# Expert weights in 4-MB units: rows of 32768 bytes over fours of slots

## The chip, the core and the metric

The kernel runs on one core of one Trainium2 chip. Its engines work in parallel and each takes its own instructions strictly in order: TensorE (PE in the profile, PEld for its weight loads), VectorE (DVE), ScalarE (ACT), GpSimd (POOL) and SyncE (SP), which here only issues DMAs. The metric is the device time of one execution in microseconds (us). Three runs of the kernel before took 1317.88 to 1318.74 us, median 1318.44 us.

## The reference, cut to what matters

A decoder layer: a mixer (a state-space branch and a gated branch), cross-attention into 256 memory tokens, and a mixture of 32 experts, each followed by a layer norm. The change concerns the experts, which hold nearly all the weights:

```python
def moe(x, w_router, b_router, w_gu, b_gu, w_down, b_down):
    ...
    top_v, top_i = lax.top_k(logits, TOP_K)          # 4 of 32 for each of 256 tokens
    top_w = jax.nn.softmax(top_v, axis=-1)
    gates = jnp.sum(jax.nn.one_hot(top_i, N_EXPERTS, dtype=f32) * top_w[..., None], axis=1)
    def expert_step(acc, p):
        wgu, bgu, wd, bd, g = p                      # 1024x2048 and 1024x1024, float32
        hgu = xt @ wgu + bgu
        gate = jnp.minimum(hgu[:, :D_EXPERT], SWIGLU_LIMIT)
        up = jnp.clip(hgu[:, D_EXPERT:], -SWIGLU_LIMIT, SWIGLU_LIMIT)
        glu = gate * jax.nn.sigmoid(SWIGLU_ALPHA * gate)
        y = ((up + 1.0) * glu) @ wd + bd
        return acc + g[:, None] * y.astype(f32), None
```

One expert has 8 MB of gate-and-up weights and 4 MB of down weights: 384 MB in all, read once.

## The kernel before

**Two stages.** The first stage (to about 390 us) computes the mixer, the attention and the router. The second runs over the experts e = 0 to 31 in pairs. For each pair, one-hot matrices pick up to 64 tokens for each expert (`gather`, L971, in four groups of two 128-row blocks). An expert then has eight steps k of `products` (L1050: four products in each, against 2 x 512 gate and 2 x 512 up columns), the bias (L1057, four short products), `swiglu` on VectorE and ScalarE (L1062 to L1066), the transpose of its result `uc` (`hidden_t`, L1075, copied to `hT` by ScalarE in L1076), and `down` (L1089, eight steps of two products). After every odd expert `scatter` (L1100) adds both results of the pair to the sum. At expert 16, `add_rest` (L930, L937) adds the biases and the residual to it. The profile counts two instructions for each product in float32.

**Overlap.** The code starts the next expert early: after `swiglu` of expert e it issues the products of k = 0 and 1 of expert e + 1 (`AHEAD = 2`), and only then `hidden_t` and `down` of e. The final order of instructions on each engine is not that of the code: a scheduler chooses it at build time, from its own estimate of when each operand is there, the weights' DMAs among them. It may put a transpose ahead of products that it expects to wait for their weights.

**Weights.** Memory holds 22 slots of 1 MB (128 partitions x 8192 bytes). 14 are in one tile, `arena`; the pairs `xhl`, `ab`, `t01` and `t23` are tiles of a pool; `d` is half of `cd`. In the first stage these slots hold activations and that stage's own weights. Each call of `expert_w` fetches a unit of 2 MB on SP's queue. The first 22 MB come as 1-MB pieces (L1023, list `FIRST`), each into a slot that the first stage has given up. After that a unit goes to the next of ten pairs of slots (`RING`, L1035), as one DMA with rows of 16384 bytes; it waits until the products that read the pair's old contents are done. `products` calls `expert_w` in every second step, `down` twice. The last expert's down weights are cut by output columns (`w_last`), and the last units come as 1-MB pieces (L1033).

SP's queue is in order, and a DMA also waits for the one eight places ahead of it, so that at most eight are under way:

```python
        name = RING[(i - len(FIRST) // 2) % len(RING)]
        ...
        if apart:
            for h in range(2):
                nc.sync.dma_start(t[:, h], src[:, h])
        else:
            nc.sync.dma_start(t, src)
```

Of the kernel before, what the change touches and what calls it, by code (L numbers as in the profile page):

```python
# [17 lines left out]
P = 128  # L18
# [31 lines left out]
def block_kernel(ctx: ExitStack, tc: tile.TileContext, a, out):  # L50
# [11 lines left out]

    arena = cp.tile([P, len(SLOTS), 2048], F32, name="arena")
    big = ctx.enter_context(tc.tile_pool(name="big", bufs=1))

    def two(tag, dt=F32):

        return big.tile([P, 2, 2048], dt, tag=tag, name=uniq(tag))

# [133 lines left out]
    def w_parts():  # L203
        t = two(("t01", "t23")[tcount[0] % 2], F32R).rearrange("p q (i c) -> p q i c", i=2)
        tcount[0] += 1
        return [[t[:, q, i] for q in range(2)] for i in range(2)]
# [122 lines left out]
    kT = bt("e0").rearrange("p (k m) -> p k m", k=KB)  # L329
    mh, ml = feat("ab")  # L330
    hs, ls = w_parts()
# [30 lines left out]
    keys(2, wk2)  # L362
    xh, xl = feat("xhl")
    for k2 in range(4):
# [18 lines left out]

    gbm = bt("g").rearrange("p (g d) -> p g d", g=2)
    gvu = two("ab")
    gv = gvu[:, 0].rearrange("p (c d) -> p c d", c=2)
    st = stats_tile(2)
# [18 lines left out]
    ygh, ygl = feat("cd")  # L406
    uT = gvu[:, 1].rearrange("p (k t) -> p k t", k=KB)

# [190 lines left out]

    ysh, ysl = feat("ab")  # L600

# [93 lines left out]
    proj_residual(hh, hl, x0, x1, st)  # L695
    xh, xl = feat("xhl")
    bg3 = bgs[:96, :].bitcast(BF16)
# [308 lines left out]
    def expert_w(src, apart=False):

        i = ucount[0]
        ucount[0] += 1
        if 2 * i < len(FIRST):  # L1010
            t = []
            for h in range(2):
                name = FIRST[2 * i + h]
                with tc.issue_after(wload[PHASE_A.index(FIRST_AFTER.get(name, ("wo", 3)))].ins):
                    if name in SLOTS:
                        t.append(bt(name))
                    elif name == "d":
                        t.append(cd[:, 1])
                    else:
                        if h == 0:  # L1020
                            both = two(name)
                        t.append(both[:, h])
                    nc.sync.dma_start(t[h], src[:, h])  # L1023
            return t
        name = RING[(i - len(FIRST) // 2) % len(RING)]
        if name in SLOTS:
            at = SLOTS.index(name)
            t = arena[:, at:at + 2, :]
        else:
            t = two(name)  # L1030
        if apart:
            for h in range(2):
                nc.sync.dma_start(t[:, h], src[:, h])  # L1033
        else:
            nc.sync.dma_start(t, src)  # L1035
        return [t[:, h] for h in range(2)]

    def gate_up(src, sel, xe, before=None, last=False):

# [38 lines left out]

    def down(src, odd, hT, y, apart=False, between=None):

        for u in range(2):
            if u and between is not None:
                between()
            w = expert_w(src(u), apart)
            for b in range(4):
                k = 4 * u + b
                for n in range(2):
                    o = 64 * (n ^ odd)
                    te.matmul(y[n][o:o + 64, :], hT[:, b, 64 * u:64 * u + 64],  # L1089
                              w[b // 2][:, b % 2 * D + n * 512:b % 2 * D + (n + 1) * 512], start=(k == 0), stop=(k == KB - 1))  # L1090

# [74 lines left out]
    def before(e, k):  # L1166
# [12 lines left out]
        if e % 2 and k == 5 and e < NE - 1:  # L1179
            p.weights()  # L1180

    def begin(e):
        xg = pairs[e // 2].xg
        current[e] = gate_up(lambda u: a["w_gu"][e, u], i96[:, e:e + 1], lambda k: xg[:, k, e % 2 * CAP:(e % 2 + 1) * CAP],
                             lambda k: before(e, k), e == NE - 1)

# [3 lines left out]
    for e in range(NE - 2):  # L1190
        products, swiglu = current.pop(e)
        for k in range(AHEAD, KB):
            products(k)
        uc = swiglu()
        begin(e + 1)
        for k in range(AHEAD):
            current[e + 1][0](k)
        hT = hidden_t(uc)
        if e == 14:
            overflow_table()  # L1200
        if e == 16:
# [6 lines left out]
        down(lambda u: a["w_down"][e, u], b, hT, y)  # L1208
# [17 lines left out]
    hTb = []  # L1226
    down(lambda u: a["w_down"][ea, u], 0, hT, y, True, lambda: hTb.append(hidden_t(uc)))
    scatter_one(y, PS[0])
    ys = None
    for q in range(4):  # L1230
        if q % 2 == 0:
            w = expert_w(a["w_last"][q // 2], True)
        new = down_piece(hTb[0], w[q % 2], q)
        if ys is not None:
            scatter_piece(ys, PS[1], q - 1, st)
        ys = new
# [5 lines left out]
    with tc.For_i(0, nx, 1):  # L1242
# [49 lines left out]
        for i in range(2):  # L1292
# [14 lines left out]
RING = FIRST[0:20:2]  # L1307

# [15 lines left out]
def arrange(inputs):  # L1324
# [33 lines left out]
    r["w_last"] = wd[NE - 1].reshape(KB, P, 4, 256).transpose(2, 1, 0, 3).reshape(2, 2, P, 2 * D).transpose(0, 2, 1, 3)  # L1358
    r["b_gu"], r["b_down"] = I["b_gu"][0], I["b_down"][0]
# [21 lines left out]
```

## Time and profile before

| | |
|---|---|
| median of three runs | 1318.44 us (1317.88 to 1318.74) |
| profiled execution | 1318.8 us |
| its span, from first to last instruction | 1317.1 us |
| TensorE busy | 1254.6 us, 95% |
| mean granted clock | 0.987 of 2.4 GHz |
| DMA, whole span | 472.00 MB, 358 GB/s |
| second stage, first product to last | 393.6 to 1305 us |

The profile shows when each instruction ran on its engine, what a waiting instruction waited for, the clock that TensorE was granted, and how busy the DMA engines were. The span lies 1.7 us under the execution's own time. A busy TensorE is one with an instruction in flight; whether it or the weights set the pace of a stretch is read from what it waits for there.

### The profile page before, as it was taken

To read this page: it belongs to the slowest core of one execution; us is meant where nothing else is said; L and a number is where in the kernel's file an instruction comes from. 1 tells how busy PE (TensorE), PEld (TensorE's weight loads), DVE (VectorE), ACT (ScalarE), POOL (GpSimd) and SP (SyncE) were. 2 spreads that over 40 slices of the span, in tenths; PEclk is the share of its full clock that TensorE was granted. 3 is DMA by queue.
4 is the path that set the end of the run, shared out by engine and by line. 5 is a ranking of instruction groups with operands and counts; after the bars stand their busy time and mean duration, and the time that the engine had idled before them with its cause. 6 is when DMAs were issued, how large, how long until landed. Compare 5 with 4: busy or idle time off the path is not lost.

```text
span 1317.1 us, 15917 instructions
## 1 busy us (share of the span) xinstructions
PE 1254.6 (95%) x6767; PEld 686.7 (52%) x6768; DVE 451.4 (34%) x795; ACT 315.6 (24%) x536; POOL 28.6 (2%) x49
## 2 busy tenths in 40 slices
PE   6999999999999999999999999999999999989896
PEld 6899899989874343343333433333343433323232
DVE  4569766687441222121221122221221212202114
ACT  4746665544531111111111111101111111101000
POOL 2110000001000000000000000000000000000000
PEclk9999999999999999999999999969999999999998
DMA  9755543576789999999999999999999999999993
GB/s 356 242 175 195 192 160 133 193 289 225 277 315 362 422 425 428 427 427 428 427 427 428 429 428 427 412 427 427 426 429 428 427 428 426 427 427 428 429 421 134
DMA packets 43930, 472.00 MB, mean 358 GB/s; under 512 B 5104, under 2 KB 6928, under 8 KB 10064
## 3 DMA queue, kind: packets, MB, share of 16 engines
q1 hardware_dynamic: 39840, 464.41, 85.8%
q10 hardware_dynamic: 4016, 6.55, 1.6%
q8 instruction: 54, 0.88, 0.3%
q14 instruction: 20, 0.16, 0.0%
HBM read 469.49 MB, written 1.05 MB: 357 GB/s over the span
## 4 chain that ended last, share of the span: by engine, by line
PE 78%; DMA 15%; DVE 3%; ACT 2%; issue 1%; POOL 0%; ACTq 0%; DVEq 0%; SPq 0%; POOLq 0%
PE gu L1050 27%; PE y L1089 14%; PE mm L255 6%; PE mm L239 5%; PE mm L238 5%; PE mm L237 5%; PE sm L971 4%; PE sm L1100 4%; DMA arena<-in_w_down_dram 3%; DMA arena<-in_w_gu_dram 3%; DMA ab<-in_w_gu_dram 3%; DMA t<-in_w_gu_dram 3%; DMA t<-in_w_down_dram 2%; PE sm L1075 1%; DVE t L181 1%
## 5 line engine op out<-in xcount | busy, mean ns | idle before, releaser
L1050 PE MATMUL gu<-arena,cd 128*64 128x512 f32 x1240 | 279.8, 594 | 4.5 <-DMA arena<-in_w_gu_dram 4.5
L1050 PEld LDWEIGHTS gu<-arena,cd 128*64 128x64 f32 x1240 | 86.6, 137 | 171.2 <-issue 157.4
L181 DVE TENSOR_TENSOR t<-arena,t 128x1024 fp32r<-128x1024 f32 (+1 forms) x111 | 131.9, 1210 | 49.6 <-ACT t L180 49.6
L1089 PE MATMUL y<-arena,hT 128*64 128x512 f32 x592 | 140.4, 615 | 5.6 <-ACT hT L1076 5.6
L180 ACT ACTIVATE t<-arena 128x1024 fp32r<-128x1024 f32 (+1 forms) x114 | 113.9, 1039 | 59.1 <-issue 18.5
L1062 DVE TENSOR_SCALAR gc<-gu 128x512 f32<-128x512 f32 x32 | 22.1, 692 | 297.3 <-PE gu L1057 297.3
L237 PE MATMUL mm<-xhl,t 128*128 128x256 f32 x384 | 110.5, 288 | 0.0
L239 PE MATMUL mm<-xhl,t 128*128 128x256 f32 x384 | 108.9, 283 | 1.5 <-DVE t L181 1.5
L238 PE MATMUL mm<-xhl,t 128*128 128x256 f32 x384 | 108.7, 283 | 0.0
L1063 ACT ACTIVATE sg<-gc 128x512 f32<-128x512 f32 x32 | 20.2, 630 | 341.7 <-DVE gc L1062 341.7
L975 DVE TENSOR_SCALAR cd<-sm,par 128x128 f32<-128x128 f32 x64 | 26.2, 410 | 210.5 <-ACT cd L973 210.2
L1105 DVE TENSOR_TENSOR cd<-sm,cd 128x512 f32<-128x512 f32 x56 | 38.7, 692 | 170.9 <-PE sm L1100 170.9
L1050 PE MATMUL gu<-t,cd 128*64 128x512 f32 x384 | 87.1, 595 | 0.0
L1089 PEld LDWEIGHTS y<-arena,hT 128*64 128x64 f32 x592 | 42.5, 140 | 84.4 <-issue 74.8
L973 ACT ACTIVATE cd<-sm,par 128x128 f32<-128x128 f32 x64 | 29.3, 457 | 227.4 <-PE sm L971 226.0
L971 PEld LDWEIGHTS sm<-pair,arena 128*128 128x128 f32 x512 | 62.0, 191 | 31.7 <-issue 27.2
L239 PEld LDWEIGHTS mm<-xhl,t 128*128 128x128 f32 x384 | 73.5, 192 | 1.7 <-DVE t L181 1.7
L971 PE MATMUL sm<-pair,arena 128*128 128x128 f32 x512 | 71.3, 285 | 3.2 <-ACT pair L989 1.8
L238 PEld LDWEIGHTS mm<-xhl,t 128*128 128x128 f32 x384 | 73.6, 192 | 0.2
L237 PEld LDWEIGHTS mm<-xhl,t 128*128 128x128 f32 x384 | 73.5, 192 | 0.2
L1100 PE MATMUL sm<-ys,pair 128*128 128x512 f32 x120 | 59.1, 615 | 10.4 <-ACT ys L1094 10.2
L1050 PE MATMUL gu<-ab,cd 128*64 128x512 f32 x208 | 48.8, 613 | 4.0 <-DMA ab<-in_w_gu_dram 4.0
(320 smaller groups left out, 1432.6 us busy)
## 6 DMA issues: line engine op xcount, KB each, us to landing
arena<-in_w_gu_dram SPq DMA_DIRECT2D x71, 2048.0 KB, 32.3
arena<-in_w_down_dram SPq DMA_DIRECT2D x35, 2048.0 KB, 30.2
arena<-in_wa_dram SPq DMA_DIRECT2D x56, 1024.0 KB, 5.0
t<-in_w_gu_dram SPq DMA_DIRECT2D x22, 2048.0 KB, 35.1
ab<-in_w_gu_dram SPq DMA_DIRECT2D x13, 2048.0 KB, 31.5
xhl<-in_w_gu_dram SPq DMA_DIRECT2D x12, 2048.0 KB, 30.1
t<-in_w_down_dram SPq DMA_DIRECT2D x12, 2048.0 KB, 30.9
arena<-in_w_gu_dram SPq DMA_DIRECT2D x13, 1024.0 KB, 7.3
```

What stands on the lines that cost most here:

```text
L180: se.activation(h, src, AF.Copy)
L181: sub_op[0] = (eng or ve).tensor_tensor(l, src, h.bitcast(F32), ALU.subtract)
L237: te.matmul(ps[:, b, :], wh, xh[:, k, :], start=(k == 0), stop=False)
L238: te.matmul(ps[:, b, :], wh, xl[:, k, :], start=False, stop=False)
L239: te.matmul(ps[:, b, :], wl, xh[:, k, :], start=False, stop=(k == KB - 1))
L255: last[0] = te.matmul(res[c], x[:, k, c * P:(c + 1) * P], w[k // 2 % 2][:, k % 2, :], start=(k == 0 and i == 0), stop=(k == KB - 1 and i = ...
L971: te.matmul(pg[:, b, :], x2[:, c, k * P:(k + 1) * P], self.t[:, 0, c, :], start=(c == 0), stop=(c == 1))
L973: se.activation(self.xg[:, k, :], pg[:, 0, :], AF.Identity, bias=b2[:, k:k + 1], scale=g2[:, k:k + 1])
L1050: te.matmul(t[64 * j:64 * j + 64, :], xe(k), ws[k][:, n * D + j * 512:n * D + (j + 1) * 512], start=(k == 0), stop=False)
L1089: te.matmul(y[n][o:o + 64, :], hT[:, b, 64 * u:64 * u + 64], w[b // 2][:, b % 2 * D + n * 512:b % 2 * D + (n + 1) * 512], start=(k == 0), ...
L1100: te.matmul(ps, PT[:, c, :], ys[n], start=True, stop=True)
L1105: ve.tensor_tensor(av, ps, av, ALU.add)
```

## The change

The weights come in units of 4 MB, with rows of 32768 bytes, into fours of neighbouring slots. `xhl` and `ab` become one tile of four slots (`four0`: xh, xl, a, b), `t01` and `t23` another (`four1`: t0 to t3), each kept through the first stage; `arena` is put in another order so that its ring slots lie in fours too. The ring has five fours. `products` fetches a unit in every fourth step (k = 0 and 4), `down` once. Expert 0 to 3 and the last units keep 2-MB pieces, and `w_last` 1-MB pieces. In the first stage the two temporaries of the gated branch move from `ab` to `h` and `j`. The list `FIRST` has another order, and the host lays the weights out accordingly.

```diff
+    four = {}
+    def fours(i, dt):
+        if (i, dt) not in four:
+            four[i, dt] = big.tile([P, 4, 2048], dt, tag=f"four{i}", name=uniq(f"four{i}"))
+        return four[i, dt]
...
-    gvu = two("ab")
-    gv = gvu[:, 0].rearrange("p (c d) -> p c d", c=2)
+    gv = bt("h").rearrange("p (c d) -> p c d", c=2)
...
-    uT = gvu[:, 1].rearrange("p (k t) -> p k t", k=KB)
+    uT = bt("j").rearrange("p (k t) -> p k t", k=KB)
...
+    def expert_w(src, n=1):
+        out = []
+        h = src.shape[1]
+        while len(out) < h:
+            i = ucount[0]
+            if i < len(FIRST):
+                m, name = 1, FIRST[i]
...
+            else:
+                m = min(n, h - len(out))
+                at = (rcount[0] + NRING - len(FIRST) % 4) % NRING
+                assert at % m == 0
+                rcount[0] += m
+                t = slots(RING[at // 4] + at % 4, m)
+                after = ExitStack()
+            ucount[0] += m
+            with after:
+                nc.sync.dma_start(t, src[:, len(out):len(out) + m])
+            out += [t[:, q] for q in range(m)]
+        return out
...
-            if k % 2 == 0:
-                ws[k], ws[k + 1] = expert_w(src(k // 2), last and k == KB - 2)
+            if k % 4 == 0:
+                ws.update(enumerate(expert_w(src(k // 4), n_rows[k // 4]), k))
...
-        for u in range(2):
-            if u and between is not None:
+        w = expert_w(src, rows)
+        for k in range(KB):
+            if k == 4 and between is not None:
                 between()
-            w = expert_w(src(u), apart)
...
+    def rows_of(e):
+        return (2, 2) if e < 4 else (4, 4)
...
+                             lambda k: before(e, k), (4, 2) if e == NE - 1 else rows_of(e))
...
-FIRST = ["e1", "k", "g", "gb", "xhl", "xhl", "w3", "w4", "e0", "x0", "ab", "ab", "w5", "w0", "w1", "w2", "t01", "t01", "t23",
-         "t23", "j", "d"]
-SLOTS = ["e1", "k", "g", "gb", "w3", "w4", "e0", "x0", "w5", "w0", "w1", "w2", "j", "h"]
+FIRST = ["e1", "k", "g", "gb", "w5", "w0", "xh", "xl", "a", "b", "e0", "x0", "w1", "w2", "j", "w3", "w4", "t0", "t1", "t2", "t3", "d"]
+SLOTS_R = ["xh", "xl", "a", "b", "t0", "t1", "t2", "t3"]
+SLOTS = ["g", "gb", "w5", "w0", "e0", "x0", "w1", "w2", "w3", "w4", "e1", "k", "j", "h"]
+RING = [8, 0, 12, 4, 16]
...
-    r["w_gu"] = wg.reshape(NE, 4, 2, P, 2 * D).transpose(0, 1, 3, 2, 4)
-    r["w_down"] = wd.reshape(NE, 2, 4, P, D).transpose(0, 1, 3, 2, 4).reshape(NE, 2, P, 2, 2 * D)
+    r["w_gu"] = wg.reshape(NE, 2, 4, P, 2 * D).transpose(0, 1, 3, 2, 4)
+    r["w_down"] = wd.reshape(NE, KB, P, D).transpose(0, 2, 1, 3).reshape(NE, P, 4, 2 * D)
```

The scheduler's order changes with the units. On TensorE, at the end of an odd expert (here 9) before: the last bias product, the next expert's steps k = 0 and 1 (eight products, two in a row), the transpose of `uc`, `down`.

```order
L1057 MATMUL gu_4737<-bgs,i_109 64x512
L1050 MATMUL gu_4850<-arena,cd_3791 64x512 x2
L1050 MATMUL gu_4851<-arena,cd_3791 64x512 x2
L1050 MATMUL gu_4850<-arena,cd_3791 64x512 x2
L1050 MATMUL gu_4851<-arena,cd_3791 64x512 x2
L1075 MATMUL sm_4862<-ident,uc_4844 128x128 x4
L1089 MATMUL y_5_4761<-t_34_4868,hT_4861 64x512
```

The same place on TensorE now (L1068 is the bias, L1086 the transpose, L1061 the products, L1098 `down`):

```order
L1068 MATMUL gu_4645<-bgs,i_109 64x512
L1086 MATMUL sm_4765<-ident,uc_4747 128x128
L1061 MATMUL gu_4753<-four_2_3895,cd_3731 64x512 x2
L1061 MATMUL gu_4754<-four_2_3895,cd_3731 64x512 x2
...
L1086 MATMUL sm_4765<-ident,uc_4747 128x128 x3
L1061 MATMUL gu_4753<-four_2_3895,cd_3731 64x512 x2
...
L1098 MATMUL y_5_4669<-arena,hT_4764 64x512
```

The first of the four transposes now stands right behind the bias, and the other three behind the next expert's k = 0 and 1; all four steps of that expert's first unit stand ahead of `down`. It is so for the odd experts 5 to 29 and for 4 and 30, 15 in all.

On TensorE at the end of an even expert (10) before: the last of the next expert's eight products, the transpose, two groups of `gather`, the transpose of the pair's weights (L988), then the first half of `down`.

```order
L1050 MATMUL gu_4949<-arena,cd_3791 64x512 x2
L1075 MATMUL sm_4967<-ident,uc_4942 128x128 x4
L971 MATMUL sm_4994<-pair_4919,arena 128x128 x4
L971 MATMUL sm_5010<-pair_4919,arena 128x128 x4
L988 MATMUL sm_5025<-ident,G_5022 128x128 x2
L1089 MATMUL y_6_4973<-arena,hT_4966 64x512
...
L971 MATMUL sm_5033<-pair_4919,arena 128x128 x4
```

The same place now (L980 is `gather`, L997 the transpose of the pair's weights):

```order
L1068 MATMUL gu_4754<-bgs,i_109 64x512
L980 MATMUL sm_4847<-pair_4818,arena 128x128 x4
L1086 MATMUL sm_4864<-ident,uc_4839 128x128 x4
L980 MATMUL sm_4889<-pair_4818,arena 128x128 x4
L980 MATMUL sm_4904<-pair_4818,arena 128x128 x3
L1061 MATMUL gu_4845<-four_2_3788,cd_3731 64x512 x2
...
L980 MATMUL sm_4904<-pair_4818,arena 128x128
L997 MATMUL sm_4919<-ident,G_4916 128x128 x2
L980 MATMUL sm_4927<-pair_4818,arena 128x128 x4
L1098 MATMUL y_6_4870<-arena,hT_4863 64x512
```

Between bias and transpose there is now one group of `gather` instead of eight products, and the last group stands right behind L997. It is so for the even experts 6 to 28, 12 in all.

On SP's queue, the first units of the ring before:

```order
L1035 DMA arena<-in_w_down_dram 128x4096 x2
L1035 DMA xhl_4057<-in_w_gu_dram 128x4096
L1035 DMA arena<-in_w_gu_dram 128x4096 x2
L1035 DMA ab_4109<-in_w_gu_dram 128x4096
L1035 DMA arena<-in_w_down_dram 128x4096 x2
```

And now:

```order
L1045 DMA arena<-in_w_gu_dram 128x4096
L1045 DMA arena<-in_w_down_dram 128x4096 x2
L1045 DMA four_2_3788<-in_w_gu_dram 128x4096 x2
L1045 DMA arena<-in_w_gu_dram 128x4096 x2
L1045 DMA four_2_3895<-in_w_down_dram 128x4096 x2
L1045 DMA arena<-in_w_gu_dram 128x4096 x2
L1045 DMA arena<-in_w_gu_dram 128x8192
```

The sixth unit goes to slots e0 and x0, which now hold steps k = 2 and 3 of expert 1; before, it went to a pair that held half of expert 0's down weights. From then on 81 units are of 4 MB.

## Rows read from the trace of the kernel before

**Rows 1.** The profile's page: busy time of the engines, and its 40 slices.
```profile
PE 1254.6 (95%) x6767; PEld 686.7 (52%) x6768; DVE 451.4 (34%) x795; ACT 315.6 (24%) x536; POOL 28.6 (2%) x49
...
GB/s 356 242 175 195 192 160 133 193 289 225 277 315 362 422 425 428 427 427 428 427 427 428 429 428 427 412 427 427 426 429 428 427 428 426 427 427 428 429 421 134
```
**Rows 2.** Chain of waits, second stage: start us, us, what (engine, output, line, instructions).
```profile
665.51 1.98 PE sm L1100 x4
...
719.40 1.98 PE sm L1100 x4
...
1104.33 38.82 DMA t<-in_w_gu_dram
...
1183.65 39.09 DMA ab<-in_w_gu_dram
...
1222.80 39.09 DMA arena<-in_w_gu_dram
```
**Rows 3.** Waits of TensorE from 393 us: us in total, times, longest us.
```profile
PE y L1089 <- ACT hT L1076: 9.7, 14, 0.7
PE gu L1050 <- DMA arena<-in_w_gu_dram: 4.5, 6, 1.2
PE gu L1050 <- DMA ab<-in_w_gu_dram: 4.0, 3, 2.1
...
PE y L1089 <- DMA t<-in_w_down_dram: 1.5, 2, 1.2
```
**Rows 4.** Timeline of TensorE, end of expert 11: start us, us, instructions [idle before <-releaser].
```profile
706.76 3.60 PE L1050 MATMUL gu<-t,cd 128*64 128x512 f32 x16
...
711.64 7.09 PE L1089 MATMUL y<-arena,hT 128*64 128x512 f32 x32 [0.69 <-ACT hT L1076]
...
745.35 1.16 PE L971 MATMUL sm<-pair,arena 128*128 128x128 f32 x8
746.44 3.65 PE L1089 MATMUL y<-arena,hT 128*64 128x512 f32 x16
```
**Rows 5.** Timeline of all engines at the last expert's end.
```profile
1279.53 1.94 PE L1089 MATMUL y<-arena,hT 128*64 128x512 f32 x8
...
1282.34 0.63 PE L1075 MATMUL sm<-ident,uc 128*128 128x128 f32 x4 [0.88 <-DVE uc L1066]
```
**Rows 6.** Timeline of VectorE, one copy of `gather`.
```profile
693.14 0.41 DVE L975 TENSOR_SCALAR cd<-sm,par 128x128 f32<-128x128 f32 x1 [4.68 <-ACT cd L973]
```
**Rows 7.** Timeline of TensorE, end of expert 16: `gather` right behind L988.
```profile
885.03 0.38 PE L988 MATMUL sm<-ident,G 128*128 128x128 f32 x2
886.02 1.16 PE L971 MATMUL sm<-pair,arena 128*128 128x128 f32 x8 [0.60 <-ACT pair L989]
```
**Rows 8.** Timeline of TensorE: its two longest waits for weights.
```profile
1173.82 5.35 PE L1050 MATMUL gu<-ab,cd 128*64 128x512 f32 x16 [2.08 <-DMA ab<-in_w_gu_dram]
...
1271.98 3.65 PE L1050 MATMUL gu<-ab,cd 128*64 128x512 f32 x16 [1.50 <-DMA ab<-in_w_gu_dram]
```
**Rows 9.** Stretches: us, busy us (instructions) of each engine, PEclk, DMA share, GB/s.
```profile
382.00:384.00 2.00, 2.00 (x14) 1.76 (x14) 0.90 (x3) 0.00 (x0) 0.00 (x0) 1.00 1.00 422
398.00:400.00 2.00, 2.00 (x12) 0.80 (x12) 0.41 (x1) 0.46 (x1) 0.00 (x0) 1.00 0.96 221
840.00:880.00 40.00, 38.94 (x136) 14.81 (x136) 14.03 (x24) 1.69 (x3) 0.00 (x0) 0.74 1.01 415
1172.00:1174.00 2.00, 0.18 (x2) 0.18 (x4) 1.81 (x4) 0.63 (x1) 0.00 (x0) 1.00 1.05 442
1174.00:1176.00 2.00, 2.00 (x6) 0.51 (x6) 0.43 (x1) 0.00 (x0) 0.00 (x0) 0.55 0.98 418
1176.00:1178.00 2.00, 2.00 (x8) 0.63 (x6) 0.00 (x0) 0.00 (x0) 0.00 (x0) 0.60 0.96 410
```
**Rows 10.** Timeline of TensorE: expert 1's k = 2 and 3; then expert 2's.
```profile
423.49 3.60 PE L1050 MATMUL gu<-arena,cd 128*64 128x512 f32 x16
...
453.75 3.22 PE L1050 MATMUL gu<-xhl,cd 128*64 128x512 f32 x13
```

More of the change, by code (lines that the diff above doesn't have):

```diff
@@ L64, in block_kernel @@
     big = ctx.enter_context(tc.tile_pool(name="big", bufs=1))
+    four = {}
[3 more added lines that the diff above has]
+        return four[i, dt]
     def two(tag, dt=F32):
-        return big.tile([P, 2, 2048], dt, tag=tag, name=uniq(tag))
+        if tag == "cd":
+            return big.tile([P, 2, 2048], dt, tag=tag, name=uniq(tag))
+        at = SLOTS_R.index(tag)
+        return fours(at // 4, dt)[:, at % 4:at % 4 + 2, :]
     def bt(tag, shape=(P, 2048)):
@@ L203, in w_parts @@
     def w_parts():
-        t = two(("t01", "t23")[tcount[0] % 2], F32R).rearrange("p q (i c) -> p q i c", i=2)
+        t = two(("t0", "t2")[tcount[0] % 2], F32R).rearrange("p q (i c) -> p q i c", i=2)
         tcount[0] += 1
@@ L329, in block_kernel @@
     kT = bt("e0").rearrange("p (k m) -> p k m", k=KB)
-    mh, ml = feat("ab")
+    mh, ml = feat("a")
     hs, ls = w_parts()
@@ L362, in block_kernel @@
     keys(2, wk2)
-    xh, xl = feat("xhl")
+    xh, xl = feat("xh")
     for k2 in range(4):
@@ L598, in ssd_b @@
         se.activation(y, zz, AF.Square, accum_out=ssq[:, i:i + 1])
-    ysh, ysl = feat("ab")
+    ysh, ysl = feat("a")
     def ssd_norm():
@@ L681, in block_kernel @@
     x1 = bt("h").rearrange("p (c d) -> p c d", c=2)
-    mh, ml = feat("ab")
+    mh, ml = feat("a")
     mem = []
@@ L695, in block_kernel @@
     proj_residual(hh, hl, x0, x1, st)
-    xh, xl = feat("xhl")
+    xh, xl = feat("xh")
     bg3 = bgs[:96, :].bitcast(BF16)
@@ L1004, in block_kernel @@
     ucount = [0]
[L1006 to L1036, printed above, removed]
@@ L1038, in gate_up, with slots @@
-    def gate_up(src, sel, xe, before=None, last=False):
+    rcount = [0]
+    def slots(i, n):
+        if i < len(SLOTS_R):
+            return fours(i // 4, F32)[:, i % 4:i % 4 + n, :]
+        i -= len(SLOTS_R)
+        return arena[:, i:i + n, :]
+    def expert_w(src, n=1):
[5 more added lines that the diff above has]
+                m, name = 1, FIRST[i]
+                if name == "d":
+                    t = cd[:, 1:2]
+                else:
+                    t = slots((SLOTS_R + SLOTS).index(name), 1)
+                after = tc.issue_after(wload[PHASE_A.index(FIRST_AFTER.get(name, ("wo", 3)))].ins)
+            else:
+                m = min(n, h - len(out))
[9 more added lines that the diff above has]
+        return out
@@ L1040, in gate_up @@
+    def gate_up(src, sel, xe, before=None, n_rows=(4, 4)):
         gp, up = pst("gu", 4), pst("gu", 4)
@@ L1077, in hidden_t, with down @@
         return hT
-    def down(src, odd, hT, y, apart=False, between=None):
-        for u in range(2):
-            if u and between is not None:
+    def down(src, odd, hT, y, rows=4, between=None):
+        w = expert_w(src, rows)
+        for k in range(KB):
+            if k == 4 and between is not None:
                 between()
-            w = expert_w(src(u), apart)
[L1085 to L1090, printed above, removed]
+            for n in range(2):
+                o = 64 * (n ^ odd)
+                te.matmul(y[n][o:o + 64, :], hT[:, k % 4, 64 * (k // 4):64 * (k // 4) + 64],
+                          w[k // 2][:, k % 2 * D + n * 512:k % 2 * D + (n + 1) * 512], start=(k == 0), stop=(k == KB - 1))
     def scatter(y, PT, first=False):
@@ L1184, in begin @@
         current[e] = gate_up(lambda u: a["w_gu"][e, u], i96[:, e:e + 1], lambda k: xg[:, k, e % 2 * CAP:(e % 2 + 1) * CAP],
-                             lambda k: before(e, k), e == NE - 1)
+                             lambda k: before(e, k), (4, 2) if e == NE - 1 else rows_of(e))
     begin(0)
@@ L1207, in block_kernel @@
             y = [pst(f"y{n}", 1) for n in range(2)]
-        down(lambda u: a["w_down"][e, u], b, hT, y)
+        down(a["w_down"][e], b, hT, y, rows_of(e)[0])
         if b:
@@ L1226, in block_kernel @@
     hTb = []
-    down(lambda u: a["w_down"][ea, u], 0, hT, y, True, lambda: hTb.append(hidden_t(uc)))
+    down(a["w_down"][ea], 0, hT, y, 2, lambda: hTb.append(hidden_t(uc)))
     scatter_one(y, PS[0])
     ys = None
+    w = expert_w(a["w_last"])
     for q in range(4):
-        if q % 2 == 0:
-            w = expert_w(a["w_last"][q // 2], True)
-        new = down_piece(hTb[0], w[q % 2], q)
+        new = down_piece(hTb[0], w[q], q)
         if ys is not None:
@@ L1278, in block_kernel @@
         hT = hidden_t(swiglu())
-        down(lambda u: a["w_down"][bass.ds(ev, 1), u].rearrange("e p h d -> p (e h) d"), 0, hT, y)
+        down(a["w_down"][bass.ds(ev, 1)].rearrange("e p h d -> p (e h) d"), 0, hT, y)
         ys = wk.tile([P, 512], F32, tag="ux", name="ysx")
@@ L1355, in arrange @@
     wg, wd = I["w_gu"][0], I["w_down"][0]
-    r["w_gu"] = wg.reshape(NE, 4, 2, P, 2 * D).transpose(0, 1, 3, 2, 4)
-    r["w_down"] = wd.reshape(NE, 2, 4, P, D).transpose(0, 1, 3, 2, 4).reshape(NE, 2, P, 2, 2 * D)
-    r["w_last"] = wd[NE - 1].reshape(KB, P, 4, 256).transpose(2, 1, 0, 3).reshape(2, 2, P, 2 * D).transpose(0, 2, 1, 3)
+    r["w_gu"] = wg.reshape(NE, 2, 4, P, 2 * D).transpose(0, 1, 3, 2, 4)
+    r["w_down"] = wd.reshape(NE, KB, P, D).transpose(0, 2, 1, 3).reshape(NE, P, 4, 2 * D)
+    r["w_last"] = wd[NE - 1].reshape(KB, P, 4, 256).transpose(1, 2, 0, 3).reshape(P, 4, 2 * D)
     r["b_gu"], r["b_down"] = I["b_gu"][0], I["b_down"][0]
```

2 lines of the change are left out of this document (1 added, 1 removed).

## The prediction

> **What bounds the kernel now.** I read the page first: TensorE is busy in 95% of the span, and the DMA rate stands near 427 GB/s from the fourteenth slice to the last but one [rows 1]. Both look full, so the chain of waits has to say which one sets the pace. From 665.51 to 719.40 us, one pair of experts, it runs over TensorE, a pair taking 53.9 us; only from 1104.33 us on does it run over transfers, in steps of 39.09 us [rows 2]. Eight transfers of 2 MB are under way at a time, so one takes 39.09 / 8 = 4.89 us, and the 24 MB of a pair 58.6 us. So TensorE is the faster of the two, lives on the 22 MB that were fetched ahead, and catches up with the stream at the end. The third view, TensorE's own waits, gives the price of that end: 4.5 + 4.0 + 1.5 = 10.0 us for weights in the whole second stage [rows 3]. The reader is to take from this that weights are not scarce until 1104 us. A microsecond that TensorE loses before that is paid in full once some 10 us of cover are used up.
>
> **Larger transfers.** Where the queue is full, 1-MB pieces (rows of 8192 bytes) come at 422 GB/s, so in 2.485 us each, and 2-MB units (16384 bytes) in 4.89 us [rows 2, 9]. Doubling the row saved 2 x 2.485 - 4.89 = 0.08 us, as a fixed time for each row would. An estimate for a 4-MB unit is then 2 x 4.89 - 0.08 = 9.70 us, and 81 units save 6.5 us of stream. No row shows 32768 bytes: if such a row is moved in two parts the saving is 0, and if it went at the rate of the 8192-byte rows the stream would be 81 x 0.16 = 13 us longer. I take 6.5, the step nearest to it. It is off the path unless the stream bounds.
>
> **Transposes behind the bias.** This is the term that decides. Before, eight products (3.60 us) stand between an expert's bias and the transpose of `uc`, and the chain gc, sg, product, uc on VectorE and ScalarE is done behind them [rows 4]. The one place of before with less between them shows the chain's length: the bias is over and `down` starts at 1279.53, the transpose has to wait until 1282.34, with `uc` named as what it waited for [rows 5]. So uc comes 2.81 us behind the bias. In the changed order, 15 experts have the transpose (or its first quarter) right behind the bias. TensorE takes instructions in order, and what is queued behind the waiting transpose is the next expert's products and `down`: it stands still for 2.81 us. 15 x 2.81 = 42.2 us. Twelve even experts have one group of `gather` in between, which takes 746.44 - 745.35 = 1.09 us [rows 4]: 12 x (2.81 - 1.09) = 20.6 us. In these, VectorE also copies half of that group between two steps of the chain, 0.41 us [rows 6], 12 x 0.41 = 4.9 us; the bounds are 0, if the copy falls into a gap of the chain, and twice that, if it waits for ScalarE's half.
>
> **Smaller terms on TensorE.** The last group of `gather` stands right behind L988's successor in 13 places instead of 4; where it does now, it waits 0.60 us [rows 7]: 9 x 0.60 = 5.4 us. In the odd experts the three late quarters of the transpose are followed by eight products before `down`, so ScalarE's copy of `hT`, now waited for 0.69 us each [rows 4], is hidden: 13 x 0.69 = 9.0 us back. If TensorE is the slower side, its waits for weights go, 10.0 us [rows 3], and with them the one drop of the clock that they caused (1.7 us, below). At the last expert the wait of 0.88 us [rows 5] goes, since eight products of `down`, twice as many, now stand ahead of that transpose: 0.9 us. Sum without the clock: 42.2 + 20.6 + 4.9 + 5.4 - 9.0 - 10.0 - 1.7 - 0.9 = 51.5 us.
>
> **The clock.** After TensorE had stood still for 2.08 us (1171.74 to 1173.82), its next eight products took 5.35 us instead of 3.65, and the granted clock was 0.55 and 0.60 of full in the two stretches that follow, that is 1.2 GHz of 2.4 for most of them; after 1.50 us of standing still the same products took 3.65 [rows 8, 9]. One drop costs 5.35 - 3.65 = 1.70 us. The 15 waits of 2.81 us are well above the one that brought the clock down: I count all, 25.5 us. The 12 of the even experts (1.72 + 0.41 = 2.13) are at its size: I count half, 10.2 us. Together 35.7; the bounds are 0 and 27 x 1.70 = 45.9. The Trainium skill, "TensorE: Matmul & The Clock Gate", section "HAM oscillation — how this bites in real kernels", describes a kernel that fell back to the half clock at every step because it waited at every step. [...]
>
> **Start of the ring.** The list of first pieces fills the same 22 slots, and the first ring unit waits, as before, for the first two steps of expert 0; the transfers stand idle until 398 us in both [rows 9]. The sixth unit, though, now waits for expert 1's steps k = 2 and 3, which end at 423.49 + 3.60 = 427.1 us [rows 10]. Five units from 398.3 on are through at 422.8; so the transfers stand idle for some 5 us (427.1 and 1 us to start). The eleventh waits likewise for expert 2's k = 2 and 3, which follow the scatter, to 457.4 or so [rows 10], while its five forerunners, from 428, are through at 452.6: again 5. Together about 10 us of stream, more than the larger units save. What covers it is the stock of fetched weights, as long as TensorE is the slower side. At the end a piece of 2 MB instead of 1 MB lies behind the last wait of `down`, 3.65 instead of 1.94 us of products [rows 5, 8]: 1.7 us, also only where the stream bounds. The moves in the first stage (the temporaries in `h` and `j`, the order of first pieces) change no count of instructions on TensorE; I cost them at 0, within one wait of 2 us either way. Around expert 16 the scheduler spreads `add_rest` among the next expert's products; before, the clock averaged 0.74 there over 40 us, 20.8 us of them at half, so 10.4 us lost [rows 9]. I take no change; the bounds are 10.4 us back and a drop of 1.70 more.
>
> **Which side bounds afterwards.** TensorE's pair becomes 53.9 + 2.81 + 1.72 + 0.41 + 0.60 - 0.69 = 58.8 us, and 60.5 to 62.2 with one or two drops of the clock. The stream's pair becomes 6 x 9.70 = 58.2. So TensorE is the slower side throughout and never waits for weights.
>
> **Sum.** 1318.8 (the profiled execution, 1.7 us above its span) + 51.5 + 35.7 = 1406.0 us; the median of the runs is 0.4 lower, so 1405.
>
> **Rivals.** First: the stalls come, but the clock stays at full speed. For it speaks that a wait of 1.50 us left the clock alone, and that 2.08 us is one case; against it, that all 27 waits are longer than this case. Time: 1318.8 + 51.5 = 1370. Second: the stalls fall where TensorE would wait for weights anyhow, and the stream bounds from early on, with its idle 10 us at the start. For it speaks that the DMA rate is flat already; against it, that TensorE waits for nothing but copies until 1104 us. It needs the added time of a pair to stay under 58.2 - 53.9 = 4.3 us; I have 4.9. Time: 1318.8 - 6.5 + 10.3 + 1.7 = 1324, still slower. Third, on the other side: the stream bounds and does not stand idle, since the slots come free sooner than I read; then the larger rows are the whole effect. It decides, like the second, from 4.3 us a pair down, and needs slots e0 and x0 free by 422 us; that they hold steps which run after `down` of expert 0 speaks against it. Time: 1318.8 - 6.5 + 1.7 = 1314. The Trainium skill, "DMA: Bandwidth & Descriptors", section "Anatomy of one DMA — SWDGE (gpsimd) path", gives each DMA of that path a fixed 2.0 us besides its bytes; an estimate by that page, were the fixed part paid one after another, is 81 x 2.0 = 162 us saved. The trace does not agree for transfers kept in a queue: eight in 39.09 us leave no room for it. Fourth: nothing measurable, if gains and stalls cancel; about 0.2%, 2.6 us, is what a measurement can tell from no change.
>
> **How the numbers follow.** Forecast with the clock 0.66, own range 1392 to 1416; full clock 0.19, 1360 to 1380; stream with idle start 0.07; faster by the larger rows 0.05; no change 0.03. The range takes in the first two cases and both bounds of the clock: 1358 to 1418. Slower by over 0.2% has 0.66 + 0.19 + 0.07, less 0.01 for its edge: 0.91; faster 0.05; the same 0.04.
>
> **What would show it.** In the profile after: TensorE waiting for `uc` some 27 times with about 2.8 us the longest, 63 to 68 us in all; a pair of 60 to 62 us; stretches at a granted clock below 1 in most pairs; no wait for weights; a DMA rate below 428 GB/s with gaps, the first near 423 us. If TensorE waits for weights as often as for `uc`, or a pair stays at 54 us, the step on the transposes is wrong. If the waits are there and the clock stays at 1.00, the first rival holds.

## The result, and the profile after

The changed kernel takes 1382.02 us (median of five runs, 1377.14 to 1383.1), the one before 1318.74 us in the runs beside it: a ratio of 1.0463, 95% interval 1.0449 to 1.0478. That is 63.3 us slower. The forecast was 1405 us with a range of 1358 to 1418: side, place and mechanism hold, the size is 23 us too large. The range that the prediction gave to this mechanism alone, 1392 to 1416, was missed by 10 us; 1382 lies closer to the upper end of the first rival (1360 to 1380), so the profile has to tell the two apart. The profiled execution took 1382.02 us, its span is 1380.3 us.

First the page of the changed kernel (busy time, and the rate in 40 slices; it answers to [rows 1]).

```profile
PE 1273.9 (92%) x6767; PEld 696.4 (50%) x6768; DVE 450.6 (33%) x795; ACT 321.3 (23%) x536; POOL 28.9 (2%) x49
...
GB/s 364 247 159 214 183 150 161 198 314 148 335 380 380 364 427 436 429 431 430 426 419 421 394 430 325 231 426 436 429 429 414 430 431 389 429 410 430 425 174 32
```

TensorE has the same instructions and 19.3 us more busy time, and it is idle for 1380.3 - 1273.9 = 106.4 us instead of 62.5, 43.9 more. The two make the 63.2 us between the spans. The flat 427 GB/s of before is gone: the transfers now wait for TensorE.

The waits of TensorE from 393 to 1305 us (us in total, times, longest) answer to [rows 3].

```profile
PE sm L1086 <- DVE uc L1077: 59.9, 26, 2.7
...
PE sm L980 <- ACT pair L998: 7.7, 13, 0.6
```

No wait for weights is left, and `uc` is waited for 26 times; with expert 30 at 1324 us it is 27 times and 62.6 us. The next rows are the timeline of TensorE at the end of an odd expert, then at an even and an odd end of a pair whose clock stayed up (start us, us, instructions, idle time before; against [rows 4, 7]).

```profile
545.92 0.60 PE L1068 MATMUL gu<-bgs,i 96*64 96x512 bf16 x4
549.26 0.33 PE L1086 MATMUL sm<-ident,uc 128*128 128x128 f32 x1 [2.74 <-DVE uc L1077]
549.52 5.35 PE L1061 MATMUL gu<-four,cd 128*64 128x512 f32 x16
...
1202.58 1.16 PE L980 MATMUL sm<-pair,arena 128*128 128x128 f32 x8
1205.53 0.66 PE L1086 MATMUL sm<-ident,uc 128*128 128x128 f32 x4 [1.79 <-DVE uc L1077]
...
1216.13 1.16 PE L980 MATMUL sm<-pair,arena 128*128 128x128 f32 x8 [0.60 <-ACT pair L998]
...
1234.35 0.33 PE L1086 MATMUL sm<-ident,uc 128*128 128x128 f32 x1 [2.75 <-DVE uc L1077]
1234.61 3.65 PE L1061 MATMUL gu<-arena,cd 128*64 128x512 f32 x16
```

The wait is 2.74 us in odd experts and 1.79 in even ones. Behind the one at 549 us the eight products take 5.35 us, behind the one at 1234 us 3.65: the same wait brought the clock down once and not the other time. Stretches of the changed kernel (us, busy us and instructions of PE, PEld, DVE, ACT, POOL; PEclk, DMA share, GB/s) show the clock there, around expert 16, and the transfers at the ring's start (against [rows 9]).

```profile
547.00:549.00 2.00, 0.00 (x0) 0.00 (x0) 1.81 (x4) 0.63 (x1) 0.00 (x0) 1.00 1.03 442
551.00:553.00 2.00, 2.00 (x8) 0.54 (x6) 0.00 (x0) 0.00 (x0) 0.00 (x0) 0.50 0.80 344
...
880.00:920.00 40.00, 37.31 (x169) 16.49 (x166) 14.49 (x26) 2.93 (x6) 0.00 (x0) 0.91 0.99 425
...
420.00:422.00 2.00, 2.00 (x12) 0.64 (x10) 0.00 (x0) 0.00 (x0) 0.00 (x0) 1.00 0.21 90
450.00:452.00 2.00, 2.00 (x12) 0.61 (x10) 0.53 (x3) 0.00 (x0) 0.00 (x0) 1.00 0.00 0
```

The transfers stand idle near 421 and 451 us while TensorE is busy throughout. Around expert 16 the clock now averages 0.91 over 40 us, where it had 0.74. Last, the chain of waits (start us, us, what): the start of `scatter` in four pairs, and one group of eight products (against [rows 2]).

```profile
628.31 1.98 PE sm L1109 x4
...
688.63 1.98 PE sm L1109 x4
...
732.21 6.37 PE gu L1061 x16
...
750.19 1.98 PE sm L1109 x4
...
808.82 1.98 PE sm L1109 x4
```

The pair to 808.82 us, in which both waits left the clock alone, takes 58.6 us; the one to 688.63, with one drop, 60.3, so 1.7 us more. In the one to 750.19 the low clock lasted longer: the products behind a wait took 6.37 us, and the pair 61.6, 3.0 us more. Before, a pair took 53.9.

### The profile page after: what moved, and what is told of

Read it like the earlier page. It is cut to its first block, busy times and chain, and to the rows that moved or that the text cites. A ratio compares the mean times of both kernels' runs of the same rounds, so it can differ in the third digit from the quotient of the medians.

```text
span 1380.3 us, 15802 instructions
## 1 busy us (share of the span) xinstructions
PE 1273.9 (92%) x6767; PEld 696.4 (50%) x6768; DVE 450.6 (33%) x795; ACT 321.3 (23%) x536; POOL 28.9 (2%) x49
## 4 chain that ended last, share of the span: by engine, by line
PE 90%; DVE 5%; ACT 3%; issue 1%; DMA 0%; ACTq 0%; DVEq 0%
PE gu L1061 34%; PE y L1098 16%; PE mm L265 8%; PE mm L248 5%; PE mm L249 5%; PE mm L247 5%; PE sm L1109 4%; PE sm L980 4%; PE sm L1086 2%; DVE gc L1073 1%; DVE gc L1076 1%; DVE uc L1077 1%; ACT sg L1074 1%; PE y L1133 1%; PE sm L946 1%; ACT ys L1103 1%
## 5 line engine op out<-in xcount | busy, mean ns | idle before, releaser
L1061 PE MATMUL gu<-arena,cd 128*64 128x512 f32 x1240 | 288.8, 610 | 0.0
L1061 PE MATMUL gu<-four,cd 128*64 128x512 f32 x800 | 194.6, 632 | 0.0
L1061 PEld LDWEIGHTS gu<-arena,cd 128*64 128x64 f32 x1240 | 87.5, 140 | 171.1 <-issue 167.4
L191 DVE TENSOR_TENSOR four<-arena,four 128x1024 fp32r<-128x1024 f32 (+1 forms) x119 | 137.9, 1169 | 83.2 <-ACT four L190 80.2
L190 ACT ACTIVATE four<-arena 128x1024 fp32r<-128x1024 f32 (+1 forms) x122 | 122.1, 1015 | 103.0 <-PE mm L248 48.9
L247 PE MATMUL mm<-four,four 128*128 128x256 f32 x496 | 142.2, 287 | 0.0
L248 PE MATMUL mm<-four,four 128*128 128x256 f32 x496 | 140.5, 283 | 0.0
L249 PE MATMUL mm<-four,four 128*128 128x256 f32 x496 | 140.5, 283 | 0.0
L1098 PE MATMUL y<-arena,hT 128*64 128x512 f32 x576 | 127.3, 594 | 0.0
L1061 PEld LDWEIGHTS gu<-four,cd 128*64 128x64 f32 x800 | 58.1, 144 | 113.4 <-issue 110.7
L247 PEld LDWEIGHTS mm<-four,four 128*128 128x128 f32 x496 | 95.1, 192 | 0.2
L248 PEld LDWEIGHTS mm<-four,four 128*128 128x128 f32 x496 | 95.1, 192 | 0.2
L249 PEld LDWEIGHTS mm<-four,four 128*128 128x128 f32 x496 | 95.0, 192 | 0.0
L1098 PE MATMUL y<-four,hT 128*64 128x512 f32 x416 | 93.0, 594 | 0.0
L980 PE MATMUL sm<-pair,arena 128*128 128x128 f32 x512 | 76.8, 296 | 10.0 <-ACT pair L998 7.7
L980 PEld LDWEIGHTS sm<-pair,arena 128*128 128x128 f32 x512 | 65.8, 200 | 35.7 <-issue 21.2
L1086 PE MATMUL sm<-ident,uc 128*128 128x128 f32 x128 | 25.6, 309 | 62.6 <-DVE uc L1077 62.6
L1098 PEld LDWEIGHTS y<-arena,hT 128*64 128x64 f32 x576 | 41.9, 137 | 77.5 <-issue 76.0
## 6 DMA issues: line engine op xcount, KB each, us to landing
arena<-in_w_down_dram SPq DMA_DIRECT2D x16, 4096.0 KB, 18.3
```

The costliest lines, as they stand in the source:

```text
L190: se.activation(h, src, AF.Copy)
L191: sub_op[0] = (eng or ve).tensor_tensor(l, src, h.bitcast(F32), ALU.subtract)
L247: te.matmul(ps[:, b, :], wh, xh[:, k, :], start=(k == 0), stop=False)
L248: te.matmul(ps[:, b, :], wh, xl[:, k, :], start=False, stop=False)
L249: te.matmul(ps[:, b, :], wl, xh[:, k, :], start=False, stop=(k == KB - 1))
L980: te.matmul(pg[:, b, :], x2[:, c, k * P:(k + 1) * P], self.t[:, 0, c, :], start=(c == 0), stop=(c == 1))
```

## The experiments

Theory: the larger unit makes the scheduler expect products to wait for weights, so it puts the transposes of `uc` ahead of them; TensorE then waits and its clock drops. Rivals: the units or the slots themselves hold TensorE back; or the waits cost, and the low clock does not.

**Order put back.** The 4-MB units stay.

```diff
+                    mm[0] = te.matmul(t[64 * j:64 * j + 64, :], xe(k), ...   # products
...
-        hT = hidden_t(uc)
+        with tc.issue_after(mm[0].ins): hT = hidden_t(uc)
```

> The changed kernel with its 4-MB units, slots and list of first pieces, but the transposes of uc put behind the next expert's k = 0 and 1 again, by an edge in the order of TensorE. Theory (the order is the cause): waits for uc fall from 62.6 us to under 3, the granted clock returns, TensorE's pair falls to about 54 us and the stream bounds, 6 x 9.7 = 58.2 us a pair. Time: before's 1318.8, less 4.3 (first product at 389.3 instead of 393.6), plus 8 (transfers idle near 422 and 449 us), plus 1.7 (last down piece of 2 MB), less 6.5 (larger rows) = 1318, range 1310 to 1326. Rival (the units are the cause, since a 4-MB unit needs four free slots): waits for uc go, but waits for weights take their place, over 20 us in all and from 600 us on, and the time stays above 1340.

Measured: 1318.58 us, ratio to before 0.9997 (0.9986 to 1.0008). Its waits for weights over the second stage:

```profile
PE gu L1061 <- DMA arena<-in_w_gu_dram: 6.4, 3, 2.2
PE gu L1061 <- DMA four<-in_w_gu_dram: 4.9, 4, 1.9
PE y L1098 <- DMA arena<-in_w_down_dram: 4.5, 4, 2.0
...
PE y L1098 <- DMA four<-in_w_down_dram: 2.5, 3, 2.0
```

No wait for `uc` is left, and the 18.3 us for weights are those of a kernel that the stream bounds. So all 63 us came with the order; the units, the slots and the list of first pieces together neither take nor give anything that can be measured (what they give and take singly comes below).

**Pieces of 2 MB, slots as changed.**

```diff
-        return (2, 2) if e < 4 else (4, 4)
+        return (2, 2)
```

> The changed kernel with pieces of 2 MB for every expert, slots and first pieces as changed; the scheduler then puts the transposes behind the next expert's products by itself. Theory (order is the cause, slots and list cost only the idle time of the transfers): no waits for uc, transfers of 4.89 us, so 6.5 us above the run with 4-MB units: 1324, range 1316 to 1330. Rival 1 (the slots and the list of first pieces hold TensorE back): above 1340. Rival 2 (a larger row saves nothing): the same time as with 4-MB units, within 2 us.

Measured: 1324.18 us, ratio 1.0047 (1.003 to 1.0063). Not a single wait for `uc`, with no edge in the order: the size of the unit alone is what moved the transposes. Why the scheduler moved them, whether because it expects a wait for the larger unit as the theory has it, no run shows. The 5.6 us above the first experiment go with the smaller rows. The rate where the queue is full, first experiment, then this one:

```profile
960.00:1100.00 140.00, 133.15 (x646) 54.57 (x644) 28.21 (x55) 19.61 (x37) 0.00 (x0) 1.00 1.00 430
```
```profile
960.00:1100.00 140.00, 133.35 (x638) 53.67 (x638) 28.58 (x55) 19.87 (x37) 0.00 (x0) 0.99 1.01 428
```

**The kernel before, with the transposes behind the bias.**

```diff
+        if e > 3:
+            last = pairs[e // 2 + 1].gather(0) if e % 2 == 0 else None
+            with tc.issue_after(last.ins) if last else ExitStack(): hT = hidden_t(uc)
         begin(e + 1)
...
+                    with tc.issue_after(tp[0].ins) if k == 0 and tp else ExitStack(): te.matmul(...)
```

> The kernel before, with its 2-MB units and slots, but the transposes of uc forced right behind the bias for experts 4 to 29 (26 places, in the even ones without a group of gather between). Theory (order is the cause): 26 waits for uc of 2.74 us = 71.2, hT's 9.7 us of waits and the 10.3 us for weights go, clock drops as in the changed kernel, about one in two waits at 2.07 us = 27, less the one of 1.7: 1318.8 + 71.2 - 20 + 25 = 1395, range 1380 to 1408; clock mean about 0.97. Rival (the stalls hurt only with 4-MB units, since with 2-MB units the stream bounds anyhow at 58.6 us a pair): 1325 to 1345.

Measured: 1402.94 us, ratio 1.0643 (1.0625 to 1.0661). The transposes alone, on 2-MB units, cost even more: no group of `gather` runs between bias and transpose in the even experts either, so 26 waits are of the long kind. They stand here together with the last expert's short one:

```profile
PE sm L1078 <- DVE uc L1069: 71.6, 27, 2.8
```

The rival, that a stream of 58.6 us a pair would hide it, falls: most pairs take 60.8 to 62.1 us.

**Waits filled with products.** `uc` comes no sooner, but TensorE has something to do.

```diff
+                for i in range(warm):       # 2 for odd experts and 30, 1 for even ones
+                    with tc.issue_after(last.ins): te.matmul(hp[0], ident, x2[:, 0, :512], start=True, stop=True)
```

> The changed kernel with one-hot-size extra products (128x512, result overwritten by the transposes) between bias and transposes: two of about 1 us for odd experts and 30, one for even ones, so that TensorE does not stand still for long but uc comes no sooner. Theory (waits 43 us and clock 20 us both pay): rest of waits for uc about 0.8 x 27 = 22 us, no or few clock drops before 1340 us, time 1382 less 14 drops' 29 us = 1353, range 1348 to 1362. Rival (the slowing is the waits alone, the low clock falls into them): time within 4 us of the changed kernel's 1382. A time above 1386 would mean that the extra products delay uc themselves.

Measured: 1336.85 us, ratio 1.0141 (1.0124 to 1.0157). One odd end (L1075 is the filler):

```profile
1194.61 1.98 PE L1075 MATMUL sm<-arena,ident 128*128 128x512 f32 x4
1197.43 0.66 PE L1092 MATMUL sm<-ident,uc 128*128 128x128 f32 x4 [0.83 <-DVE uc L1083]
```

1.98 + 0.83 = 2.8 us from bias to transpose, as without filler. Yet the span is 45.1 us shorter. The mean granted clock is 0.995 instead of 0.974: (1 - 0.974) x 1380.3 - (1 - 0.995) x 1335.2 = 29.2 us of clock. The other 16 us I had not expected: a pair at full clock takes 57.2 us here and 58.6 in the changed kernel. The scheduler ordered the gathers otherwise (waits for `pair` in L980 fall from 7.7 to 2.4 us, and the even transposes come 0.2 us sooner); the rest I have not taken apart. So the rival without a price for the clock falls, and the clock's share is about 29 us, not all 45. The changed kernel's own trace agrees: read in stretches of 4 us, its low clock behind 14 waits adds up to 28.7 us lost.

**Ring's start mended.** On top of the order: 2-MB pieces up to expert 7, asked for two steps at a time, and w3, w4 ahead of t0.

```diff
+                if rcount[0] < 62: at = {12: 16, 14: 12, 16: 14}.get(at, at)
...
-            if k % 4 == 0:
-                ws.update(enumerate(expert_w(src(k // 4), n_rows[k // 4]), k))
+            if k % (m := n_rows[k // 4]) == 0:
+                ws.update(enumerate(expert_w(src(k // 4)[:, k % 4:k % 4 + m], m), k))
```

> The changed kernel with the transposes put back as in the first experiment, and with the ring started as in the kernel before: 2-MB pieces up to expert 7 that are asked for two steps at a time (so down of expert 0 goes to e0, x0, w1, w2), and w3, w4 ahead of t0 in the ring's first three laps. Theory (the idle of the transfers near 422 and 449 us, 3 and 6 us, costs time once the stream bounds): no gap of over 3 us after 400 us, so 9 us less than the first experiment's 1318.6, plus 1 for twelve fewer 4-MB units: 1311, range 1306 to 1316. Rival (the stream stands idle there because the stock of 22 MB is full, and would stand idle a little later instead): 1317 to 1321, with gaps of the same length behind 450 us.

Measured: 1310.72 us, ratio 0.994 (0.9927 to 0.9953): it is faster than both kernels. The same stretches of the first experiment and of this one:

```profile
420.00:424.00 4.00, 4.00 (x24) 1.88 (x22) 0.02 (x1) 0.46 (x1) 0.00 (x0) 1.00 0.26 57
448.00:452.00 4.00, 4.00 (x17) 1.32 (x18) 1.78 (x4) 0.00 (x0) 0.00 (x0) 1.00 0.08 33
452.00:456.00 4.00, 4.00 (x22) 1.36 (x20) 0.00 (x0) 0.00 (x0) 0.00 (x0) 1.00 0.60 197
```
```profile
420.00:424.00 4.00, 4.00 (x24) 1.84 (x22) 0.00 (x0) 0.04 (x1) 0.00 (x0) 1.00 1.01 434
448.00:452.00 4.00, 4.00 (x16) 1.28 (x16) 2.10 (x5) 0.00 (x0) 0.00 (x0) 1.00 1.04 442
452.00:456.00 4.00, 4.00 (x22) 1.31 (x20) 0.00 (x0) 0.00 (x0) 0.00 (x0) 1.00 0.94 377
```

The gaps are gone and did not come back later; they cost about 8 us once the stream bounds. In the changed kernel, where TensorE bounds, they are off the path.

**The same with 2-MB pieces to the end.**

```diff
-        return (2, 2) if e < 8 else (4, 4)
+        return (2, 2)
```

> The same as the run with the ring's start mended, but with 2-MB pieces to the end. Theory (a 4-MB unit saves about 0.08 us over two of 2 MB): 428 GB/s instead of 431, so 69 x 0.08 = 5.6 us above that run: 1317, range 1312 to 1321. Rival (the larger row saves nothing, and the 5.6 us between the first two experiments came from the order): the same time within 2 us.

Measured: 1314.69 us, ratio 0.9967 (0.9955 to 0.998), so 4.0 us above the run before, less than the 5.6 expected but beyond the rival's 2. With the 2-MB units the scheduler also brings back the waits for `hT` (9.8 us instead of 1.4) and the half clock at expert 16 (11.9 us lost), so the row is not all that differs; but the stream bounds both, and its rate from 460 to 1260 us is 427 GB/s here and 430 there. Of the 8.5 us that the best version gains on before, 4.0 go with the larger rows and 4.5 are there without them: the first scatter comes at 445.60 us here, 4.3 us sooner than before.

**The two temporaries alone, in the kernel before.**

```diff
-    gvu = two("ab")
-    gv = gvu[:, 0].rearrange("p (c d) -> p c d", c=2)
+    gv = bt("h").rearrange("p (c d) -> p c d", c=2)
...
-    uT = gvu[:, 1].rearrange("p (k t) -> p k t", k=KB)
+    uT = bt("j").rearrange("p (k t) -> p k t", k=KB)
```

> The kernel before with one part of the change alone: the two temporaries of the gated branch in h and j instead of ab. Theory (this makes the first stage 4.4 us shorter, since they no longer wait for the tile ab): first scatter at 445.5 instead of 449.9 us, the stream starts 4.4 us sooner and bounds the end: 1319.5 - 4.4 = 1315, range 1313 to 1317. Rival (the first stage is shorter through the new list of first pieces): first scatter at 449.9 and the time of before, within 1.5 us.

Measured: 1318.92 us, ratio 1.000 (0.999 to 1.001); the first scatter, in the kernel before at 449.87 us, comes at 450.13:

```profile
450.13 3.96 PE L1099 MATMUL sm<-ys,pair 128*128 128x512 f32 x8 [0.59 <-ACT ys L1093]
```

In the changed kernel it comes at 445.44. The theory falls: the shorter first stage has another cause, in the new slots, the order of the first pieces or the scheduler's order. It stays open.

**add_rest spread, and add_rest's waits filled.** Both start from the kernel before with the transposes behind the bias, where the clock is low at expert 16. The first puts the next expert's products among those of `add_rest`, as the changed kernel has them; the second leaves the order and adds a product on either side of `norm_row`'s first products, where the kernel before waits 0.53 us twice (with the transposes behind the bias, only the second of these waits is left).

```diff
+        if e == 16:
+            add_rest(acc)          # first: ahead of begin(17), whose k = 0 waits for norm_row's products
         begin(e + 1)
```
```diff
+    def fill(last):                # second: behind the gates' transposes and behind norm_row's products
+        with tc.issue_after(last.ins):
+            te.matmul(fy[0], ident, x2[:, 0, :512], start=True, stop=True)
```

> The kernel before with the transposes forced right behind the bias, as in the third experiment (1402.9 us, TensorE the slower side, 20.5 us of half clock at expert 16, that pair 83.1 us against 60.8), and with add_rest's products now spread among the next expert's k = 0 and 1 as the changed kernel has them. Theory (the order of add_rest took 10 us of clock, which the changed kernel got back): half clock at expert 16 at most 7 us, that pair about 72 us, the time 1403 - 10 = 1393, range 1388 to 1397. Rival (the 20.5 us fall into time in which TensorE has little to do anyhow): within 3 us of 1403.

> The third experiment's kernel (1402.9 us, half clock for 20.5 us in add_rest at expert 16), with one extra 128x512 product (about 1 us, its result overwritten by down) in each of add_rest's two waits of 0.53 us, in the order of before otherwise. Theory (the two short waits, one right behind the other, let the clock fall, and the stretch of add_rest does not bring it back until down's row of products): no half clock there, that pair about 73 instead of 83.1 us, 1403 - 10 + 1 = 1394, range 1389 to 1398. Rival (the products with 32 rows bring the clock down by themselves): half clock as before, 1403 to 1406.

Measured: 1403.09 us, ratio 1.0628 (1.0606 to 1.0651), so the first misses; and 1395.05 us, ratio 1.0569 (1.0543 to 1.0594), so the second gains 7.9 us by the medians and 10 by the ratios, where 9 were expected. The pair at expert 16 takes 83.2 us without either edit, 84.9 with the first and 72.0 with the second. The two waits of the kernel before, then TensorE at expert 16 and the clock from 900 to 920 us, in the kernel without either edit, then in the two (L930 and L933 are `add_rest`'s products, L937, L939 and L946 `norm_row`'s, L940 in the last the filler):

```profile
852.44 2.05 PE L937 MATMUL sm<-gr,ident 32*128 32x128 f32 x16 [0.53 <-ACT hT L1076]
855.01 1.09 PE L930 MATMUL sm<-bd,gT 32*128 32x512 f32 x2 [0.53 <-PE sm L937]
```
```profile
901.45 1.09 PE L930 MATMUL sm<-bd,gT 32*128 32x512 f32 x2 [0.53 <-PE sm L937]
...
900.00:920.00 20.00, 19.47 (x49) 7.37 (x49) 9.90 (x16) 0.00 (x0) 0.00 (x0) 0.57 1.01 428
```
```profile
895.45 0.66 PE L1080 MATMUL sm<-ident,uc 128*128 128x128 f32 x4 [2.69 <-DVE uc L1071]
896.86 2.69 PE L939 MATMUL sm<-gr,ident 32*128 32x128 f32 x16 [0.53 <-ACT hT L1081]
...
898.00:900.00 2.00, 2.00 (x10) 1.53 (x9) 1.71 (x3) 0.00 (x0) 0.00 (x0) 0.52 1.01 434
900.00:920.00 20.00, 20.00 (x40) 6.65 (x38) 7.92 (x13) 0.00 (x0) 0.00 (x0) 0.50 1.00 426
```
```profile
898.90 1.02 PE L940 MATMUL y<-arena,ident 128*128 128x512 f32 x2
899.85 2.04 PE L946 MATMUL sm<-gr,ident 32*128 32x128 f32 x16
901.83 1.13 PE L940 MATMUL y<-arena,ident 128*128 128x512 f32 x2
...
900.00:920.00 20.00, 20.00 (x90) 8.64 (x92) 10.37 (x17) 0.46 (x1) 0.00 (x0) 1.00 1.00 426
```

In the first edit the wait of 2.69 us stands right ahead of `add_rest`, and one of 0.53 us ahead of `norm_row`'s products. The clock is full until 898 us, falls within those products (0.52 from 898 to 900) and stays low through the rest, though TensorE is busy all 20 us. In the second the same work as without the edit, in the same order, with two products of full size put in, runs at full clock. So both runs fit that a wait, or a stretch of 32-row products with a wait in it, brings the clock down there, and that the mixed work behind does not bring it back. Which of the two it is (the wait alone, or both together) was not taken apart, nor whether the two products help by filling waits or by being full products.

## Why the prediction came out right, step by step

**Larger transfers.** Right in kind: 430 instead of 428 GB/s. A unit takes 4.194 / 0.430 = 9.75 us by that rate, not 9.70, so it saves about half of the 0.08 us counted; by the runs it is 0.06 to 0.07 (4.0 us over 69 units, 5.6 over 81). Off the path in the changed kernel, as said. The Trainium skill, "DMA: Bandwidth & Descriptors", section "Anatomy of one DMA — SWDGE (gpsimd) path", gives a DMA issued by GpSimd a fixed 2.0 us. On SyncE's queue, with DMAs queued up, no such saving shows: units twice as large saved 4.0 us, where an estimate by that page, paid one after another for 69 DMAs fewer, is 138 us.

**Transposes behind the bias.** Right: 15 waits of 2.74 us (2.81 was taken from [rows 5]) and 12 of 1.79 make 62.6 us, against 67.7. Of the 5.1 us too much, 1.0 lies in the long waits and 4.1 in the even ones, where 2.13 us were counted: VectorE's copy was mis-sized. `uc` comes 1.16 + 1.79 = 2.95 us behind the bias there, 0.2 us later than in odd experts, where 0.41 was counted; that is within the bound of 0.

**Smaller terms.** `gather` behind L997: 7.7 - 1.8 = 5.9 us (5.4). hT's waits: all 9.7 us gone (9.0). Waits for weights: all 10.3 us gone (10.0). What failed here is the first stage, 0 within 2 us: it became 4.4 us shorter, as the first scatter shows, 3.2 us of it idle time of TensorE. Together TensorE's idle time grew by 43.9 us where 53.2 were counted; the 5.1 and the 3.2 are most of the difference.

**The clock.** This is the term with the largest error: the clock was to cost 35.7 - 1.7 = 34.0 us, and TensorE's busy time grew by 19.3. The waits' own share was nearer: 29.2 us by the run with filled waits. 14 of the 27 waits are followed by slowed products, 10 of 15 long and 4 of 12 short ones, where 21 were counted, but three of the drops (experts 11, 14 and 16) lost 3.4 us of clock each instead of 1.7. What I had put at 0, with a bound of 10.4 us back, was `add_rest`, and here that step failed: the 10.4 us of clock that before lost at expert 16 came back (0.91 over 40 us, and this with a drop of its own behind `uc`). The changed order puts eight products behind the transposes and more of them between `norm_row`'s products and `add_rest`'s own, and of its two waits of 0.53 us one of 0.32 is left. That this is what brought the clock back is argued: spreading the products alone did not do it in the last experiments, two more products of full size beside the wait did, for 8 to 10 us. The two errors, 6.5 and 10.4, are 2.2 more than the 14.7 that the term was off; the traces, read in stretches of 4 us, have these at the kernel's end, where 7.1 us of clock are lost from 1350 us on and before 4.8 from 1304 on. With the 9.3 us of idle time the 14.7 make the 24 between the counted 87.2 and the measured 63.2. The two terms erred on the same side, so the place within the range owes nothing to errors that cancel; it does owe something to the width of the range, which takes in the full clock as well. The Trainium skill, "TensorE: Matmul & The Clock Gate", section "HAM oscillation — how this bites in real kernels", describes a kernel whose clock fell at every one of its steps, behind waits longer than the ones here; here it fell at 14 of 27, so counting a drop at each (45.9 us, the prediction's bound) would have been further off.

**The start of the ring and the side that bounds.** Right: idle near 421 and 451 us, about 8 us in all (10 counted), no wait for weights, a plain pair of 58.6 us (58.8 counted). Wrong: the transfers do not stand idle until 398 us as before; from 392 to 396 us they slow to 234 and 287 GB/s, where before they stood at 37 and 0 from 394 to 398. That is off the path here too.

**The rivals.** Full clock (1370) falls with 14 drops; the bounding stream (1324, 1314) with the missing waits for weights. Where the order is put back, the stream does bound, and 1318.58 us is 5 less than the second rival's sum: it lacked the shorter first stage and counted 10 us of idle transfers for 8. The forecast itself is 1406.0 - 0.4 = 1405.6, written as 1405.

## What to carry to other kernels

A change of a transfer's size can act through the scheduler: read first which instructions changed places, and price what a waiting instruction holds up behind it on its engine. When a change to transfers slows a kernel, pin the old order of the engines before judging it; here that turned 63 us lost into nothing, and mending the ring's start turned it into 8.5 us gained. Count the clock in both directions: a new order can also take away a stretch at half clock that was there before.

## What was not expected of the hardware

A stretch of mixed products that keeps TensorE busy can stay at half clock: 0.50 from 900 to 920 us in the run with `add_rest` spread and 0.57 without either edit, against 1.00 with the same order and two full products put in. A wait of 0.53 us behind 2 us of 32-row products went with a drop there, while 5 of 15 waits of 2.74 us behind full products left the clock alone. Rows of 32768 bytes came at 430 GB/s, of 16384 at 428.
